# Experts' passes gathered in pairs from the first one, and what was spread over the first pass moved ahead of it

## The chip, the cores and the metric

The kernel runs on one core of a Trainium2 chip, in one launch. The metric is device time in microseconds (us) of one execution, from the first instruction to the last with what lies around them.

## The reference, cut to what matters

Two layers over 512 tokens of 1024 channels, all in float32. Each layer has a token mixer (layer 0 a Conformer convolution module of 31 taps, layer 1 a short gated convolution of 3 taps) and then a mixture of 32 experts in 4 groups: the best group, and in it the best two experts of each token. Both sublayers are wrapped in the same way:

```python
h = x * (1 + scale(c)) + shift(c)
x = layer_norm(ALPHA * x + (1 + gate(c)) * sublayer(h))
# the mixture's sublayer, with the tokens sorted by expert:
hid = silu(xblk @ w_gate[e]) * (xblk @ w_up[e])     # 1024 -> 512
y[tok] += weight * (hid @ w_down[e])                # 512 -> 1024
```

Every expert is used, so all its three matrices of 2 MB are read: 403 MB in the two layers, of 485 MB read in all.

## The kernel before

**Passes.** A layer's experts are taken in 14 passes of 128 slots (`PASSES`): a pass holds one to four experts in blocks of 32 slots, `(2, 2)` being two experts of 64 slots each. The experts are put on these places by their number of tokens (`perm`, L1062), but for experts 0 and 1, which always make pass 0, so that its weights can be loaded before the routing is known. Passes 1 and 13 have four experts, pass 2 one, pass 7 three, the others two.

**What a pass does** (L1214 on). A one-hot matrix of tokens against slots (`onehot`, L996) gathers the tokens: TensorE multiplies channels by tokens with it (`gather`, L1039), 16 products for two of the eight channel chunks, and ACT (L1043) and DVE (L1045) write the result with the mixture's scale and shift. Then 16 steps `t` of gate and up products (L1271), silu, four transposes (L1330), down products (L1346) in two halves `u`. The slots' routing weights come from four float32 products of the one-hot with `Wd` (`slot_weights`, L1132), and the one-hot's transpose from four transposes with a copy on ACT (`cmat`, L1122, L1125). With this transpose the next pass adds the result to the tokens (`combine`, L1150 and DVE L1142), two of its eight pieces at t = 4, 8, 12 and after.

**Gathers.** Pass 0 is gathered alone, from the float32 tokens in X (L1033). Passes 1 and 2, 3 and 4, ... 11 and 12 are gathered in pairs of 256 slots and pass 13 alone, both from a split of the tokens into a rounded high part `nh` (ACT L961) and the rest `nl` (DVE L957), in the faster float32r. Pass 0 is thus also where the four low parts are made, where all four gathers of the first pair stand (`ahead`, L1319), and where the mixture's scale and shift are turned into the other order of channels that the split has (`by_rows`, L275): two matrices built on POOL and DVE and eight products on TensorE (L292).

**Weights.** A ring of six buffers of 2 MB; SP issues the next unit's transfer when a buffer has been released (`done`, `pump`). A unit of pass 0 (`u_first`) holds gate and up of both experts for two chunks of channels, so that t runs gate, up, gate, up; in the other passes (`u_pass`) a unit holds four chunks of one matrix of two experts. A step's release stands after t = 3, 7, 11, 15 and after each half of the down products. The numbers of the experts from pass 1 on reach SP's registers by `ids` (L1089).

**The order of the work** is written out by hand: each engine runs its instructions in program order, the ones of `by_rows` and the DMA issues of ACT among them. Before pass 13, `beyond` (L1212) holds a branch for experts with more tokens than slots; it isn't taken, but every engine passes it.

**The mixer's end** (`Out.run`, L569): the output product in three float32r products for each k (L484 to L486), for its weights a high part on ACT and a low part on DVE (`fold`, `low`: L552, L558), then for each of four token groups q the layer norm (`ln`), transposes (`turn`, L895), copies (L903) and router products (`logits`, L910), and `choose` on DVE.

Of the kernel before, what the change touches and what calls it, by code (L numbers as in the profile page):

```python
# [62 lines left out]
def trunk_kernel(ctx: ExitStack, tc: tile.TileContext, x, c, ada_w, ada_b, a_w_in, a_b_in, a_w_dw, a_b_dw,  # L63
# [115 lines left out]
    def u_first(i, u):  # L179
        def f():  # L180
            t = R([128, 2, 2, 2, 512])
            for s, e in enumerate(experts(i, 0)):
                for z, w in enumerate((e_w_gate, e_w_up)):
                    nc.sync.dma_start(t[:, s, :, z], w[i, e, u * 256:(u + 1) * 256, :]
                                      .rearrange("o (k p) n -> p (o k) n", p=128))
            return t
        return f


# [18 lines left out]
    for i in range(DEPTH):  # L208
# [66 lines left out]
    def by_rows(aff, off):  # L275
        u, spread8 = W([128, 512]), W([128, KD, 2, 8])
        t8, div8, m8, mod8 = u[:, :240], u[:, 240:480], u[:, 480:481], u[:, 488:496]

        G.iota(t8, pattern=[[-8, 240]], base=8 * 112, channel_multiplier=1, **IOTA)
        V.tensor_scalar(div8, t8, 0.0, None, op0=OP.is_ge)  # L280
        V.scalar_tensor_tensor(div8, t8, 8.0, div8, op0=OP.is_lt, op1=OP.mult)
        V.tensor_mul(t8, t8, div8)
        V.tensor_reduce(m8, t8, axis=AX.X, op=OP.add)
        V.tensor_scalar(mod8, slot[:, :8], m8, None, op0=OP.is_equal)
        for z, a in enumerate((aff, off)):
            V.tensor_tensor(spread8[:, :, z], bc(a[:, :, None], [128, KD, 8]), bc(mod8[:, None, :], [128, KD, 8]),
                            op=OP.mult)

        def finish():
            p = P("b")  # L290
            for k in range(KD):
                PE.matmul(p[:, :16], div8[:, 112 - 16 * k:240 - 16 * k], spread8[:, k].rearrange("p z j -> p (z j)"),  # L292
                          start=k == 0, stop=k == KD - 1)
            r = T([128, 2, 8], F32, "aff8")
            S.activation(r.rearrange("p z j -> p (z j)"), p[:, :16], AF.Copy)
            return r
        return finish
# [242 lines left out]
    class Out:  # L540
# [28 lines left out]
        def run(self, uT, pre, uh, ul, extra, turn, copies, logits, choose, fill):  # L569
# [45 lines left out]
            for q in range(NQ):  # L615
# [226 lines left out]
    fold_rest()  # L842
    res = Out(grow, False)
# [27 lines left out]
    for i in range(DEPTH):  # L871
# [76 lines left out]
        res.run(uT, pre, nh, nl, None if i else add_bias, turn, copies, logits, choose, flex)  # L948


        def tokens(q):
            qs = slice(q * 128, (q + 1) * 128)
            return nh[:, :, qs], nl[:, :, qs], X[:, q, :].rearrange("p (n k) -> p k n", k=KD)

        def tokens_low(q):
            hi, lo, x = tokens(q)
            V.tensor_sub(lo, x, hi.bitcast(F32))  # L957

        for q in range(NQ):
            hi, lo, x = tokens(q)  # L960
            S.activation(hi, x, AF.Copy)  # L961
# [39 lines left out]
        def single(g, at, dt):  # L1001
            t = W([128, NQ, 128], dt)
            onehot(t, g, at)
            return t, None

        def pair(Q, at):
            if Q == NP // 2:
                return single(NP - 1, at, F32R)
            t = [W([128, 2, 256], F32R) for _ in range(2)]
            for h in range(2):  # L1010
                for j in range(2):
                    onehot(t[h][:, :, j * 128:j * 128 + 128], 2 * Q - 1 + j, at[:, 2 * h:2 * h + 2])
            return t

        def oh(Q, q, j=None):
            if ohs[Q][1] is None:
                return ohs[Q][0][:, q, :]
# [3 lines left out]
        def xe(Q, k, j=None):  # L1021
            r = xes[Q][k // 4][:, k % 4, :]
            return r if j is None or Q % (NP // 2) == 0 else r[:, j * 128:j * 128 + 128]

        def gather(Q, k0):
            p = P("c", (128, 2, 256))
            n = 128 if Q % (NP // 2) == 0 else 256
            for k in (k0, k0 + 1):  # L1030
                for q in range(NQ):
                    if Q == 0:
                        PE.matmul(p[:, k - k0, :n], X[:, q, k * 128:(k + 1) * 128], oh(Q, q), start=q == 0, stop=q == NQ - 1)  # L1033
                        continue
                    o = oh(Q, q)
                    if n == 128:
                        o = bc(o[:, None, :], [128, 2, 128])
                    for part, src in enumerate((nh, nl)):
                        PE.matmul(p[:, k - k0], src[:, k, q * 128:(q + 1) * 128], o, start=q == 0 and part == 0,  # L1039
                                  stop=q == NQ - 1 and part == 1)  # L1040
            affe, offe = maps[min(Q, 1)]
            k = k0
            S.activation(xe(Q, k), p[:, 0, :n], AF.Identity, bias=offe[:, k:k + 1], scale=affe[:, k:k + 1])  # L1043
            k = k0 + 1
            V.tensor_scalar(xe(Q, k), p[:, 1, :n], affe[:, k:k + 1], offe[:, k:k + 1], op0=OP.mult, op1=OP.add)  # L1045

        maps = [(aff, off)]

        ohs = [single(0, VW[:, 0], F32)]
        xes = [[W([128, 4, 128]) for _ in range(2)]]  # L1050

# [10 lines left out]
        V.tensor_scalar(perm, rank, kc[:, 1:2], None, op0=OP.is_equal)  # L1062

# [16 lines left out]

        t = by_expert(0)
        gather(0, 0)
        Vd = by_place(t, "Vd")

# [5 lines left out]

        nbf = W([1, 2, NE, 8])
# [26 lines left out]

        def cmat(ohq, C=None):
            p = P("c")  # L1120
            for q in range(NQ):
                PE.transpose(p[:, q * 128:(q + 1) * 128], ohq(q), ident)  # L1122
            if C is None:
                C = W([128, 512], F32R)
            S.activation(C, p, AF.Copy)  # L1125
            return C

        def slot_weights(ohq, e, kind):
# [4 lines left out]
            w = T([128, 5], F32, "ws", 4)  # L1133
            if n == 1:
                V.tensor_copy(w[:, 4:5], p[:, :1])
            else:
                V.scalar_tensor_tensor(w[:, :n], p[:, :n], 1.0, side[kind], op0=OP.mult, op1=OP.mult,
                                       accum_out=w[:, 4:5])
            return w[:, 4:5]
# [14 lines left out]
        def block(e, rest, eid, tiles):  # L1154
# [4 lines left out]
            w = slot_weights(lambda q: t[:, q, :].bitcast(F32), e, (4,))  # L1159
            cmat(lambda q: t[:, q, :].bitcast(F32), C)  # L1160
# [411 lines left out]
```

## Time and profile before

| | |
|---|---|
| three runs: median; lowest to highest | 3024.08 us; 1514.51 to 7848.31 us |
| the profiled execution: time, span | 1515.81 us, 1513.7 us |
| mean granted TensorE clock | 0.971 of 2.4 GHz |
| busy: PE, DVE, ACT, POOL | 94%, 48%, 23%, 17% of the span |
| passes 5 and 6 of layer 0: first gate product | 454.7 and 486.1 us |
| layer 0: experts' first gate product to last down product | 272.2 to 761.0 us |
| layer 1: the same | 1003.1 to 1492.7 us |

The span in 40 slices of 37.8 us (tenths; 9 is 90% or more), with what the DMA engines moved:

```profile
PE   5999889999999999998899989999899999999975
DVE  2699987532324333232157877563233333333315
DMA  8954435879999999999994655257999999999984
GB/s 296 396 204 171 167 111 175 323 296 421 419 378 405 404 421 420 421 421 418 357 279 153 203 200 178 105 223 282 423 421 415 402 384 421 421 421 420 421 360 156
```

The experts of layer 0 fill slices 8 to 20, those of layer 1 slices 27 to 39. TensorE is busy nearly everywhere; the DMA engines come to a ceiling of 421 GB/s in the experts' stretches alone. Where both are full, the rows of the releases and of the waits have to tell which sets the pace.

### The profile page before, as it was taken

To read this page: it belongs to the slowest core of one execution; us is meant where nothing else is said; L and a number is where in the kernel's file an instruction comes from. 1 tells how busy PE (TensorE), PEld (TensorE's weight loads), DVE (VectorE), ACT (ScalarE), POOL (GpSimd) and SP (SyncE) were. 2 spreads that over 40 slices of the span, in tenths; PEclk is the share of its full clock that TensorE was granted. 3 is DMA by queue.
4 is the path that set the end of the run, shared out by engine and by line. 5 is a ranking of instruction groups with operands and counts; after the bars stand their busy time and mean duration, and the time that the engine had idled before them with its cause. 6 is when DMAs were issued, how large, how long until landed. Compare 5 with 4: busy or idle time off the path is not lost. (4 is left out here: it accounts for less than half of the span.)

```text
span 1513.7 us, 21337 instructions
## 1 busy us (share of the span) xinstructions
PE 1416.6 (94%) x8424; PEld 769.3 (51%) x8424; DVE 725.2 (48%) x1298; ACT 341.3 (23%) x583; POOL 264.2 (17%) x275
## 2 busy tenths in 40 slices
PE   5999889999999999998899989999899999999975
PEld 3444467544544445443277777865354444444422
DVE  2699987532324333232157877563233333333315
ACT  1465565220111011110061222232001110011101
POOL 1399942050000000000025142002200000000002
PEclk8999999999999999999999999999999999999978
DMA  8954435879999999999994655257999999999984
GB/s 296 396 204 171 167 111 175 323 296 421 419 378 405 404 421 420 421 421 418 357 279 153 203 200 178 105 223 282 423 421 415 402 384 421 421 421 420 421 360 156
DMA packets 118851, 488.72 MB, mean 323 GB/s; under 512 B 12227, under 2 KB 45515, under 8 KB 71627
## 3 DMA queue, kind: packets, MB, share of 16 engines
q1 hardware_dynamic: 114443, 486.82, 81.4%
q8 instruction: 71, 1.16, 0.3%
q0 software_dynamic: 128, 0.04, 0.2%
q10 hardware_dynamic: 4160, 0.30, 0.2%
q14 instruction: 49, 0.40, 0.1%
HBM read 485.02 MB, written 2.10 MB: 322 GB/s over the span
## 5 line engine op out<-in xcount | busy, mean ns | idle before, releaser
L1271 PE MATMUL pa<-ring,w 128*32 128x512 f32 (+2 forms) x2624 | 430.6, 605 | 25.8 <-DMA ring<-in_e_w_up_dram 12.4
L1142 DVE TENSOR_TENSOR X<-X,pb 128x512 f32<-128x512 f32 x208 | 133.9, 683 | 263.8 <-PE pb L1150 263.2
L1271 PEld LDWEIGHTS pa<-ring,w 128*32 128x32 f32 (+2 forms) x2624 | 118.0, 120 | 273.5 <-issue 242.8
L1346 PE MATMUL pa<-ring,w 128*32 128x512 f32 (+2 forms) x1312 | 208.8, 601 | 8.7 <-DMA ring<-in_e_w_down_dram 7.1
L1346 PEld LDWEIGHTS pa<-ring,w 128*32 128x32 f32 (+2 forms) x1312 | 60.8, 120 | 133.4 <-issue 113.3
L1150 PE MATMUL pb<-w,w 128*128 128x512 f32 x416 | 128.2, 429 | 0.0
L765 PE MATMUL pa<-RB,ring 128*128 128x512 f32 x256 | 117.3, 616 | 4.8 <-DMA ring<-in_a_w_in_dram 2.7
L1366 DVE SCALAR_TENSOR_TENSOR w<-pa,ws,w 128x512 f32<-128x512 f32 x56 | 41.8, 750 | 163.3 <-PE pa L1346 160.7
L1150 PEld LDWEIGHTS pb<-w,w 128*128 128x128 f32 x416 | 71.0, 189 | 95.4 <-issue 81.8
L710 POOL TENSOR_TENSOR w<-w,w 128x512 f32<-128x512 f32 x80 | 104.8, 1309 | 57.1 <-ACT w L708 51.5
L1125 ACT ACTIVATE w<-pc 128x512 fp32r<-128x512 f32 x28 | 16.7, 597 | 429.6 <-PE pc L1122 429.6
L1039 PE MATMUL pc<-w,RB 128*128 128x256 f32 x448 | 111.4, 288 | 0.0
L1039 PE MATMUL pc<-w,RC 128*128 128x256 f32 x448 | 108.6, 278 | 0.0
L481 POOL TENSOR_TENSOR RC<-w,RB 128x512 fp32r<-128x512 f32 x8 | 10.9, 1382 | 440.0 <-ACT RB L480 440.0
L1039 PEld LDWEIGHTS pc<-w,RB 128*128 128x128 f32 x448 | 84.5, 189 | 2.6 <-issue 1.6
L1039 PEld LDWEIGHTS pc<-w,RC 128*128 128x128 f32 x448 | 84.1, 188 | 1.1
L765 PEld LDWEIGHTS pa<-RB,ring 128*128 128x128 f32 x256 | 49.4, 197 | 67.9 <-issue 62.4
L480 ACT ACTIVATE w<-w 128x512 fp32r<-128x512 f32 x58 | 36.6, 631 | 208.9 <-DVE w L1366 208.9
L724 DVE SCALAR_TENSOR_TENSOR pb<-RC,w,pb 128x512 f32<-128x512 f32 x126 | 83.6, 745 | 0.0
L1407 POOL TENSOR_TENSOR X<-X,w 128x512 f32<-128x512 f32 x3 | 4.9, 1619 | 428.9 <-ACT X L1406 428.9
L486 PE MATMUL pa<-RB,w 128*128 128x512 f32 x168 | 68.7, 409 | 8.8 <-DVE w L481 8.8
L1045 DVE TENSOR_SCALAR w<-pc,aff 128x256 f32<-128x256 f32 (+1 forms) x56 | 29.4, 525 | 91.3 <-ACT w L1043 91.3
(350 smaller groups left out, 1830.2 us busy)
## 6 DMA issues: line engine op xcount, KB each, us to landing
ring<-in_e_w_down_dram SPq DMA_DIRECT2D x120, 1024.0 KB, 15.6
ring<-in_e_w_gate_dram SPq DMA_DIRECT2D x120, 1024.0 KB, 12.1
ring<-in_e_w_up_dram SPq DMA_DIRECT2D x120, 1024.0 KB, 16.7
ring<-in_ada_w_dram SPq DMA_DIRECT2D x14, 2048.0 KB, 11.5
ring<-in_ada_w_dram SPq DMA_DIRECT2D x10, 1536.0 KB, 6.3
ring<-in_b_w_in_dram SPq DMA_DIRECT2D x24, 512.0 KB, 6.3
ring<-in_a_w_in_dram SPq DMA_DIRECT2D x8, 1024.0 KB, 8.0
ring<-in_e_w_gate_dram SPq DMA_DIRECT2D x16, 512.0 KB, 6.3
```

Of the source, the lines that this page charges most:

```text
L480: S.activation(hi, x, AF.Copy)
L486: PE.matmul(p, al, bh, start=False, stop=stop)
L710: G.tensor_add(vp, vp, z)
L724: V.scalar_tensor_tensor(t if j == TAPS - 1 else acc[n % 2], a, wj, acc[n % 2], op0=OP.mult, op1=OP.add)
L765: PE.matmul(p, w[:, k, h, s], hT[:, k, :], start=k == 0, stop=k == KD - 1)
L1039: PE.matmul(p[:, k - k0], src[:, k, q * 128:(q + 1) * 128], o, start=q == 0 and part == 0, stop=q == NQ - 1 and part == 1)
L1045: V.tensor_scalar(xe(Q, k), p[:, 1, :n], affe[:, k:k + 1], offe[:, k:k + 1], op0=OP.mult, op1=OP.add)
L1142: V.tensor_add(half(q, d), half(q, d), p)
L1150: PE.matmul(p, C[:, q * 128:(q + 1) * 128], ys[d][z], start=z == 0, stop=z == 1)
L1271: PE.matmul(pgu[z][a:b, :], xe(Q, k, j)[:, a:b], w[s][:, t % 4, :] if g else tiles[-1][:, s, k % 2, z, :], start=k == 0, stop=k == KD - 1)
L1346: PE.matmul(pd[d][a:b, :], hT[:, (2 * u + f) * 128 + a:(2 * u + f) * 128 + b], w[s][d][:, f, :], start=u + f == 0, stop=u + f == 2)
L1366: V.scalar_tensor_tensor(ys[d], pd[d], ws, GF[d], op0=OP.mult, op1=OP.mult)
```

## The change

Pass 0 is gathered with pass 1 as a pair, 2 with 3, and so on to 12 with 13, all from the split tokens. For that, pass 0's weights get the layout of the others (`u_first` goes), the low and high parts are made at the mixer's end and in the routing (`hook`), and pass 1's half of the first one-hot, which needs `Vd`, is built before the first gather. `by_rows` runs once for each layer at the mixer's end: two transposes, a copy on ACT and 16 small transfers issued by ACT. `slot_weights` and `cmat` become `slots_of`: one product for each token group in float32r gives the weights in two parts and each slot's token number, and DVE builds the transposed one-hot by comparing token numbers.

```diff
-    def u_first(i, u): ...
-            if g == 0:
-                todo += [u_first(i, u) for u in range(4)] + [u_pass(i, g, 4 + u) for u in range(2)]
-            elif g < NP - 1:
+            if g < NP - 1:
                 todo += [u_pass(i, g, j) for j in range(3 * n)]
...
     def by_rows(aff, off):
-        u, spread8 = W([128, 512]), W([128, KD, 2, 8])
...
+        p = P("b")
+        t = W([8, 2, 128])
         for z, a in enumerate((aff, off)):
+            PE.transpose(p[:8, z * 128:(z + 1) * 128], a, ident)
+        S.activation(t.rearrange("k z c -> k (z c)"), p[:8, :256], AF.Copy)
+        r = T([128, 2, 8], F32, "aff8")
+        for z in range(2):
             for k in range(KD):
+                S.dma_start(r[16 * k:16 * k + 16, z, :], t[k:k + 1, z, :].rearrange("o (a j) -> o a j", j=8))
+        return r[:, 0], r[:, 1]
...
                 ln(q, (lambda: copies(q - 2)) if q >= 2 else None)
+                if q < 3:
+                    hook("high", q)
             turn(2)
             copies(2)
             logits(0)
             logits(1)
+            hook("low", 0)
...
             turn(3)
             copies(3)
+            hook("high", 3)
+            hook("low", 1)
             logits(2)
             logits(3)
...
     fold_rest()
+    maps = by_rows(aff, off)          # layer 0
     res = Out(grow, False)
...
                 fold_router(1, rw, aff, off)()
+                maps = by_rows(aff, off)          # layer 1
                 res = Out(grow, True)
...
-        ohs = [single(0, VW[:, 0], F32)]
+        ohs = [pair(0, VW[:, 0], (0,))]
...
         V.tensor_scalar(perm, rank, kc[:, 1:2], None, op0=OP.is_equal)
+        hook("low", 2)
...
         t = by_expert(0)
-        gather(0, 0)
+        flex.finish()
+        if i == 0:
+            side_ada.finish()
         Vd = by_place(t, "Vd")
+        pair(0, Vd, (1,), ohs[0])
+        hook("low", 3)
...
         V.tensor_copy(ids[i], pid[:1, :NE])
+        gather(0, 0)
...
-        def cmat(ohq, C=None): ...
-        def slot_weights(ohq, e, kind): ...
+        def slots_of(ohq, e, kind, C=None):
             n = len(kind)
             p = P("c")
             for q in range(NQ):
-                PE.matmul(p[:, :n], ohq(q), Wd[:, q, e:e + n], start=q == 0, stop=q == NQ - 1)
+                PE.matmul(p[:, :4 * n], ohq(q), Wd[:, q, 4 * e:4 * e + 4 * n], start=q == 0, stop=q == NQ - 1)
...
+            V.tensor_copy(w[:, 9:10], p[:, 2:3])
+            if C is None:
+                C = W([128, 512], F32R)
+            for q in range(NQ):
+                V.tensor_scalar(C[:, q * 128:(q + 1) * 128], slot, 128.0 * q, w[:, 9:10], op0=OP.add, op1=OP.is_equal)
+            return w[:, 8:9], C
...
         for g, kind in enumerate(PASSES):
-            Q, j = (g + 1) // 2, (g + 1) % 2
+            Q, j = g // 2, g % 2
...
-                z, k = (t % 2, t // 2) if g == 0 else (t // 4 % 2, t // 8 * 4 + t % 4)
+                z, k = t // 4 % 2, t // 8 * 4 + t % 4
...
-                    if t in (1, 5, 9):
-                        gather(0, t // 4 * 2 + 2)
-                    if t in (2, 4, 6, 8):
-                        tokens_low(t // 2 - 1)
-                    if t == 3:
-                        rows8 = by_rows(aff, off)
...
+                    if t in (1, 4, 6):
+                        gather(0, {1: 2, 4: 4, 6: 6}[t])
...
             def ahead(n):
-                if Q < NP // 2:
...
-                    for k0 in (2 * n,) if Q == 0 else (4 * j + 2 * n,):
-                        gather(Q + 1, k0)
+                if Q + 1 < NP // 2:
+                    gather(Q + 1, 4 * j + 2 * n)
...
                         t = by_expert(1)
-                        ahead(2)
-                        Wd = by_place(t, "Wd")
-                        C = cmat(ohq)
+                        Wd = places(t)
                     else:
-                        ws = slot_weights(ohq, FIRST[g], kind)
-                        ahead(3)
+                        ws, C = slots_of(ohq, FIRST[g], kind)
```

`places` makes `Wd` with four columns for an expert: the weight's high and low part, and the token's number twice.

## Rows read from the trace of the kernel before

**Rows 1.** Windows: us, busy PE, PEld, DVE, ACT, POOL, clock, DMA share, GB/s
```profile
415.00:520.00 105.00, 105.00 (x740) 47.69 (x743) 36.81 (x68) 12.26 (x21) 0.00 (x0) 1.00 0.97 394
520.00:715.00 195.00, 188.55 (x1236) 87.54 (x1229) 65.02 (x121) 20.42 (x36) 0.00 (x0) 0.99 1.01 421
1140.00:1250.00 110.00, 110.00 (x781) 51.21 (x780) 39.20 (x75) 12.82 (x22) 0.00 (x0) 1.00 0.98 399
```

**Rows 2.** Timeline of SP: start, length, the issue of weights (two transfers a unit)
```profile
278.07 0.89 SPq L174 DMA_DIRECT2D ring<-in_e_w_gate_dram  x2
322.69 2.01 SPq L174 DMA_DIRECT2D ring<-in_e_w_up_dram  x4
1052.40 1.33 SPq L174 DMA_DIRECT2D ring<-in_e_w_up_dram  x2
```

**Rows 3.** Timeline of SP, around the branch of layer 1
```profile
1435.67 0.86 SPq L174 DMA_DIRECT2D ring<-in_e_w_gate_dram  x2
1453.16 2.38 SPq L174 DMA_DIRECT2D ring<-in_e_w_up_dram  x4
```

**Rows 4.** Timeline of PE in pass 5: slots' weights, transposes, two gather products
```profile
469.62 0.95 PE L1132 MATMUL pc<-Wd,w 128*128 128x2 f32 x8
470.43 0.63 PE L1122 MATMUL pc<-ident,w 128*128 128x128 f32 x4
...
474.75 0.28 PE L1039 MATMUL pc<-w,RB 128*128 128x256 f32 x1
474.87 0.28 PE L1039 MATMUL pc<-w,RC 128*128 128x256 f32 x1
```

**Rows 5.** Timeline of DVE in layer 0: perm; a low part; four one-hots
```profile
268.19 0.23 DVE L1062 TENSOR_SCALAR w<-rank,r_kc 32x32 f32<-32x32 bf16 x1
...
277.02 2.02 DVE L957 TENSOR_TENSOR RC<-X,RB 128x1024 fp32r<-128x1024 f32 x1
...
290.56 1.41 DVE L996 TENSOR_TENSOR w<-slot,Vd 128x256 fp32r<-128x256 f32 x4
```

**Rows 6.** Timeline of PE in pass 0, layer 0: two steps; by_rows
```profile
272.24 1.94 PE L1271 MATMUL pa<-ring,w 128*64 128x512 f32 x8
...
292.48 1.96 PE L292 MATMUL pb<-w,w 128*128 128x16 f32 x16
```

**Rows 7.** Timeline of ACT at layer 0's mixer end: copies; high parts
```profile
249.43 1.06 ACT L903 ACTIVATE w<-pb 128x512 f32<-128x512 f32 x2
...
257.21 8.03 ACT L961 ACTIVATE RB<-X 128x1024 fp32r<-128x1024 f32 x4
```

**Rows 8.** Timeline of PE there: turn(2)
```profile
250.75 1.03 PE L895 MATMUL pb<-ident,X 128*128 128x128 f32 x8
```

**Rows 9.** Timeline of PE: the end of an idle time in layer 0's mixer
```profile
228.25 0.79 PE L484 MATMUL pb<-w,RB 128*128 128x512 f32 x1 [3.00 <-ACT RB L574]
```

**Rows 10.** Window around it
```profile
223.00:234.00 11.00, 7.62 (x18) 5.43 (x19) 9.44 (x11) 6.72 (x12) 8.18 (x6) 0.53 0.70 251
```

**Rows 11.** Timelines: small transfers' issues on ACT and SP
```profile
148.78 0.42 ACTq L259 DMA_DIRECT2D w<-in_r_w_group_dram  x1
149.24 0.59 ACTq L260 DMA_DIRECT2D w<-in_r_w_expert_dram  x1
...
3.59 0.29 SPq L233 DMA_DIRECT2D w<-in_a_ln_g_dram  x1
```

**Rows 12.** Timelines of PE and ACT, layer 0: router product; silu
```profile
185.79 3.37 PE L267 MATMUL pb<-w,affB 128*128 128x36 f32 x16 [1.30 <-DVE affB L464]
...
193.49 0.81 ACT L860 ACTIVATE w<-w,colP 128x512 f32<-128x512 f32 x1 [4.36 <-DVE w L859]
```

**Rows 13.** The same of layer 1: fold(0) on ACT; router product on PE
```profile
920.31 1.15 ACT L552 ACTIVATE w<-ring 128x512 fp32r<-128x512 f32 x2
...
931.36 1.87 PE L267 MATMUL pb<-w,affB 128*128 128x36 f32 x16
```

**Rows 14.** DMA issues: count, size, median us to landing
```profile
w<-in_r_w_group_dram ACTq DMA_DIRECT2D x2, 16.0 KB, 2.5
```

More of the change, by code (lines that the diff above doesn't have):

```diff
@@ L176, in u_pass @@
         return f
[L179 to L187, printed above, removed]
     def u_last(i, d):
@@ L566, in early, with run @@
             self.u[k] = t
-        def run(self, uT, pre, uh, ul, extra, turn, copies, logits, choose, fill):
+        def run(self, uT, pre, uh, ul, extra, turn, copies, logits, choose, fill, hook):
             def u(k):
@@ L945, in by_group, with hook @@
             return t.rearrange("p q (g e) -> p q g e", g=NG)
-        res.run(uT, pre, nh, nl, None if i else add_bias, turn, copies, logits, choose, flex)
-        def tokens(q):
+        def hook(what, q):
             qs = slice(q * 128, (q + 1) * 128)
[L953 to L961, printed above, removed]
+            hi, lo, x = nh[:, :, qs], nl[:, :, qs], X[:, q, :].rearrange("p (n k) -> p k n", k=KD)
+            if what == "high":
+                S.activation(hi, x, AF.Copy)
+            else:
+                V.tensor_sub(lo, x, hi.bitcast(F32))
+        res.run(uT, pre, nh, nl, None if i else add_bias, turn, copies, logits, choose, flex, hook)
         cnt = P("b")
@@ L999, in onehot, with pair @@
                 o += n * c
[L1001 to L1009, printed above, removed]
+        def pair(Q, at, passes=(0, 1), t=None):
+            t = t or [W([128, 2, 256], F32R) for _ in range(2)]
             for h in range(2):
-                for j in range(2):
-                    onehot(t[h][:, :, j * 128:j * 128 + 128], 2 * Q - 1 + j, at[:, 2 * h:2 * h + 2])
+                for j in passes:
+                    onehot(t[h][:, :, j * 128:j * 128 + 128], 2 * Q + j, at[:, 2 * h:2 * h + 2])
             return t
         def oh(Q, q, j=None):
-            if ohs[Q][1] is None:
-                return ohs[Q][0][:, q, :]
             r = ohs[Q][q // 2][:, q % 2, :]
@@ L1022, in xe @@
             r = xes[Q][k // 4][:, k % 4, :]
[L1023 removed]
+            return r if j is None else r[:, j * 128:j * 128 + 128]
         def gather(Q, k0):
+            if k0 == 0:
+                xes.append([M([128, 4, 256]) for _ in range(2)])
             p = P("c", (128, 2, 256))
[L1029 removed]
             for k in (k0, k0 + 1):
                 for q in range(NQ):
[L1032 to L1037, printed above, removed]
                     for part, src in enumerate((nh, nl)):
[L1039 removed]
+                        PE.matmul(p[:, k - k0], src[:, k, q * 128:(q + 1) * 128], oh(Q, q), start=q == 0 and part == 0,
                                   stop=q == NQ - 1 and part == 1)
[L1041 removed]
+            affe, offe = maps
             k = k0
[L1043 removed]
+            S.activation(xe(Q, k), p[:, 0], AF.Identity, bias=offe[:, k:k + 1], scale=affe[:, k:k + 1])
             k = k0 + 1
[L1045 to L1050 removed]
+            V.tensor_scalar(xe(Q, k), p[:, 1], affe[:, k:k + 1], offe[:, k:k + 1], op0=OP.mult, op1=OP.add)
+        xes = []
+        ohs = [pair(0, VW[:, 0], (0,))]
         rk = W([NE, 3, NE])
@@ L1079, in by_place, with places @@
             return d
+        def places(t):
+            p = P("a", (128, NQ, 128))
+            for q in range(NQ):
+                PE.matmul(p[:, q, :NE], t[:, q * 128:(q + 1) * 128], perm, start=True, stop=True)
+            n = W([128, NQ, NE])
+            G.iota(n, pattern=[[128, NQ], [0, NE]], base=0, channel_multiplier=1, **IOTA)
+            d = W([128, NQ, 4 * NE], F32R)
+            z = d.rearrange("p q (e z) -> p q e z", z=4)
+            V.tensor_copy(z[:, :, :, 0], p[:, :, :NE])
+            V.tensor_sub(z[:, :, :, 1], p[:, :, :NE], z[:, :, :, 0].bitcast(F32))
+            V.tensor_copy(z[:, :, :, 2], n)
+            V.tensor_copy(z[:, :, :, 3], n)
+            return d
         t = by_expert(0)
-        gather(0, 0)
+        flex.finish()
+        if i == 0:
+            side_ada.finish()
         Vd = by_place(t, "Vd")
+        pair(0, Vd, (1,), ohs[0])
+        hook("low", 3)
         pid = P("a")
@@ L1245, in trunk_kernel @@
                     o += wide
[L1246 removed]
+            ohq = lambda q: oh(Q, q, j)
             if g == NP - 1:
@@ L1264, in trunk_kernel @@
             for t in range(2 * KD):
-                z, k = (t % 2, t // 2) if g == 0 else (t // 4 % 2, t // 8 * 4 + t % 4)
-                if t % 4 == 0 and g == 0:
-                    tiles.append(unit())
-                elif t % 4 == 0:
+                z, k = t // 4 % 2, t // 8 * 4 + t % 4
+                if t % 4 == 0:
                     w = [piece(t // 4 * ns + s) for s in range(ns)]
@@ L1319, in ahead @@
             def ahead(n):
-                if Q < NP // 2:
-                    first = g == max(0, 2 * Q - 1)
-                    if first and n == 0:
-                        xes.append([M([128, 4, 256]) if Q + 1 < NP // 2 else W([128, 4, 128]) for _ in range(2)])
-                    for k0 in (2 * n,) if Q == 0 else (4 * j + 2 * n,):
-                        gather(Q + 1, k0)
+                if Q + 1 < NP // 2:
+                    gather(Q + 1, 4 * j + 2 * n)
             ahead(0)
@@ L1371, in trunk_kernel @@
             pend = (C, ys)
-            if j == 1 and Q + 2 <= NP // 2:
+            if j == 1 and Q + 2 < NP // 2:
                 ohs.append(pair(Q + 2, Vd))
```

58 lines of the change are left out of this document (12 added, 46 removed).

## Prediction

> **What bounds the kernel now.** I read the windows by stage first. In the experts' stretches the DMA engines have a ceiling of 421 GB/s: they hold it for the 195 us of layer 0's passes 6 to 13, with TensorE nearly full beside them, while in the earlier passes 3 to 6 TensorE is full without a gap and the DMA engines fall to 394 GB/s (layer 1: 399) [rows 1]. So two limits lie close together. A pass of two experts is 12.6 MB, 29.9 us at the ceiling; TensorE's own time for one is some 31.4 us, the distance from pass 5 to pass 6 in the table. Passes 3 to 6 are TensorE's, the rest is the transfers': pass 7 with its three experts uses up the ring's lead, and from there no faster TensorE ends a layer sooner. What the transfers lose is small: 105 x (1 - 394/421) = 6.7 us in layer 0, 110 x (1 - 399/421) = 5.7 us in layer 1 [rows 1].
>
> The queue of SP shows how a layer starts. The first buffer is released at 278.07, a step of pass 0; but the transfers come to the ceiling only with the releases at 322.69 (layer 1: 1052.40), when pass 1's first four steps are done and two buffers come free at once [rows 2]. Before that a buffer comes free more slowly than a transfer of 5 us lasts, so those early releases may move without moving the end; the time that counts is pass 1's. At a layer's end SP stands at the branch: it issued its last unit before it at 1435.67 and the next at 1453.16, when all that was under way had landed [rows 3]. From there the rest is fixed: 12.6 MB and the last products. A layer's time is thus: when pass 1 releases, plus the stream at 421 GB/s, plus what TensorE holds the stream back in passes 3 to 6, plus a fixed tail. Outside the experts' stretches the mixers' chains count in full.
>
> **The passes.** The slots' weights and the transposes take 1.4 us of TensorE in a pass [rows 4]. Four float32r products take their place; a gather's follow each other by 0.12 us with the same 128 columns to load [rows 4], so 0.5 us, and 0.9 us is saved. The copy on ACT goes to DVE as four comparisons and two small instructions, about 1.2 us by the one-hots' price [rows 5]; DVE is 35% busy there [rows 1], and the next pass's combine, the first to read the result, comes after the down products. Nothing for that; without the cover 1.2 us a pass. Over passes 1 to 6 TensorE gains 5.4 us, which the stream can use as far as it was held back. In passes 7 to 13 the same 0.9 us, and the two gathers that pass 12 loses, end in a longer wait for weights: nothing. Only behind the last landing of layer 1 does the 0.9 us count once more.
>
> **The start of the experts.** Before, the first products stand at 272.24 [rows 6], and their gather needed no `perm`. After it, DVE has behind `perm` (done at 268.4) a low part (2.0), small additions and a copy (0.9, by the 0.2 to 0.3 us of such instructions), two one-hots (0.7) and another low part (2.0) [rows 5], to 274.0. The last products of the gather wait for that one: 1.2 us more, 0.7 us for the eviction, so 275.9, 3.7 us late. In layer 0 one more wait: the high part of q = 2 (8.03/4 = 2.0 us) now stands on ACT ahead of the copies of 249.43, and turn(2) at 250.75 needs the banks that they empty [rows 7, 8]: 1.9 us on the routing. In layer 1 ACT has that room; its low parts cost about 0.5 us there. Since TensorE idles longer before the first gather, I add 1.7 us for a stretch at the lower clock, as around an idle time of 3 us before, where the mean fell to 0.53, most of it at 1.2 GHz instead of 2.4 [rows 9, 10]. And t = 2 now waits for its own eviction, 0.7 us. Sum: 8.0 us in layer 0, 6.8 us in layer 1. Pass 0 then gives back the products of `by_rows` (2.0) [rows 6], two of four gathers of the next pair (32 x 0.12 = 3.8), and 0.9 of slots' work, with 0.6 us of `flex` transposes that fall into the wait in layer 0: 7.3 and 6.7 us. So pass 1's release comes 0.7 us later in layer 0 and 0.1 us later in layer 1. Bounds: 3 us either way, as the lower clock and DVE's order fall. The stream's gain is then the smaller of what it lost and what TensorE gave: 5.4 - 0.7 = 4.7 us in layer 0, and 5.3 us in layer 1.
>
> **The map's transfers.** Two transposes, a copy, then 16 issues on ACT, which runs in order. Nothing in the trace is a 512-byte transfer across partitions; the nearest are ACT's own issues, 0.42 and 0.59 us long and 0.46 apart, and SP's of 4 KB at 0.29 [rows 11]. I take 0.40 us each with the gap, nearest to ACT's shorter one, so 6.4 us; the ends 0.33 and 0.63 give 5.3 and 10.1 us. In layer 0 the router product ends at 189.2; transposes and copy to 190.0, issues to 196.4, fold(0) behind them 1.1, and silu starts at 197.5 instead of 193.49 [rows 12, 13]. DVE and ACT hand each other every k from there, and DVE hardly rests until the output product's last k: 4.0 us late, all on the path. In layer 1 it is worse. ACT was ahead there: it did fold(0) at 920.31, 11 us before the router product ended at 933.2 [rows 13]. Now its copy waits for that product's PE queue, so fold(0) starts at 933.2 + 0.8 + 6.4 = 940.4, and DVE's low part, which until now came some 0.5 us after the router product, follows at 941.0: 7.2 us late, and TensorE, idle for that long, comes back at the lower clock as in the same rows: 1.3 us more. 8.5 us.
>
> The transfers must land too: the Trainium skill, "DMA: Bandwidth & Descriptors", section "Rules for kernel authors", says to coalesce many small transfers, since under 64 KB one pays mostly overhead, which its section on the anatomy of one DMA puts at about 2.0 us each. The trace has 2.5 us to landing for ACT's 16 KB [rows 14], but the next issue came 0.46 us after it [rows 11]: the overhead overlaps. By the row the 16 cost 6.4 us; one after the other they would cost 16 x 2.5 = 40 us. Landed they are needed only at the first gather, some 60 us later.
>
> **The sum**, against the profiled execution of 1515.8 us (span 1513.7 and 2.1 around it): layer 0 +4.0 - 4.7; layer 1 +8.5 - 5.3 - 0.9: 1517.4, say **1517 us**. The median of the three runs, 3024 us, is twice that execution and not the kernel's own time; the lowest, 1514.51, agrees with it. I forecast no change that can be measured: a difference under 2% is about what a measurement of this kernel can't tell from none.
>
> **Rivals.**
> 1. *The early releases count, each of them.* If the stream ran at the ceiling from the first release on, the whole delay would pass: 8.0 + 6.8 - 0.8 = 14 us, 1531 us. For it: the first transfers do come later. Against it: the ceiling is reached only from 322.69 on [rows 2]. 0.12.
> 2. *The issues on ACT are hidden*, as small transfers cost ACT's queue little, or the chains behind have slack: without 12.5 us, 1505 us. Against it: no slack in DVE's row of work. 0.13.
> 3. *TensorE is the bound throughout.* Then all its savings count: 0.9 x 28 + the float32 gathers, 4 x 2.0 x 2, + 2.0 x 2 of by_rows, 45 us less; with 12.5 us of issues 1483 us. Against it: 421 GB/s for 195 us. 0.03.
> 4. *Slower: ACT's transfers go one by one*, each waiting out a landing of 2.5 us [rows 14]: by_rows then holds ACT 40 us in each layer, 33.6 us more than counted, 1517 + 67 = 1584 us. It decides from about 1.3 us for an issue on (16 x 2 x 0.9 more makes 29 us). Against it: the 0.46 us between two issues [rows 11]. 0.05. The Trainium skill's rule on small transfers points this way; with its 2.0 us in place of 2.5 this rival would give 1568 us, an estimate from that page.
>
> My forecast has 0.64, with its own spread: 5 us down (issues at 0.33, DVE's chain with slack), 13 us up (issues at 0.63, 3 us at each start). Rivals 1 and 2 fall at its ends, so the range is 1502 to 1533, with rivals 3 and 4 and some 0.1 outside. Faster by over 2% (under 1485) 0.04, slower (over 1546) 0.06, the rest no change.
>
> **What would show it.** Right: 16 issues on ACT some 0.4 us apart behind the router product, with silu 4 us and layer 1's first low part 7 us late; the first release in layer 0 6 to 8 us late and pass 1's within 1 us; middle passes of 30.5 us in the stretch that fell to 394 GB/s, now near 421; longer waits for weights from pass 8 on. Wrong: middle passes that stay at 31.4 us because DVE's new work holds the next pass; transfers of the map that land one by one; or the stream under 421 GB/s after pass 7, which would make TensorE the bound.

## The result, and the profile after

The changed kernel takes 1526.34 us in the median of four runs (1525.19 to 1528.89). Of the four runs of the kernel before beside it two are far longer than one execution (3024.08 and 7848.31 us); the other two took 1513.87 and 1514.51 us. By these two the change costs 12.2 us, a ratio of 1.0080; the ratio on record is 1.0087, 95% interval 1.0064 to 1.0109. So it is slower by 0.8 to 0.9%, clear of noise. I had forecast 1517 us, a sum of 1.6 us more than before, and no change that can be measured. The profiled execution took 1526.11 us, 10.3 more than the 1515.81 of before; spans 1524.3 and 1513.7.

The map's transfers first (the map is the mixture's scale and offset, which `by_rows` turns into the other order of channels). ACT's timeline in layer 0 (start, length, engine, line, operation, tiles; in brackets the idle time before and what ended it):

```profile
189.85 0.37 ACT L267 ACTIVATE w<-pb 8x256 f32<-8x256 f32 x1 [1.85 <-PE pb L266]
190.25 10.42 ACTq L271 DMA_DIRECT2D aff<-w  x16
200.72 1.15 ACT L527 ACTIVATE w<-ring 128x512 fp32r<-128x512 f32 x2 [10.50 <-DMA aff<-w]
201.78 0.80 ACT L841 ACTIVATE w<-w,colP 128x512 f32<-128x512 f32 x1
```

The 16 issues hold ACT for 10.42 us, 0.65 each, not the 6.4 us of my sum. `fold(0)` (L527) stands behind them, and the first silu (L841) comes at 201.78 instead of 193.49 [rows 12]. The output product ends 8.6 us later against the router product's start; its last products, before and after:

```profile
250.52 0.39 PE L486 MATMUL pa<-w,RC 128*128 128x512 f32 x1
```

```profile
259.12 0.40 PE L461 MATMUL pa<-w,RC 128*128 128x512 f32 x1
```

In layer 1 it is the same, on ACT, on DVE (the low part; the first line is the kernel before) and on PE:

```profile
939.25 10.40 ACTq L271 DMA_DIRECT2D aff<-w  x16
949.70 1.15 ACT L527 ACTIVATE w<-ring 128x512 fp32r<-128x512 f32 x2 [10.48 <-DMA aff<-w]
```

```profile
933.75 1.29 DVE L558 TENSOR_TENSOR w<-ring,w 128x512 fp32r<-128x512 f32 x2
```

```profile
950.36 1.29 DVE L533 TENSOR_TENSOR w<-ring,w 128x512 fp32r<-128x512 f32 x2 [11.23 <-ACT w L527]
```

```profile
936.66 1.87 PE L254 MATMUL pb<-w,affB 128*128 128x36 f32 x16
951.42 0.80 PE L459 MATMUL pb<-w,w 128*128 128x512 f32 x1 [12.67 <-ACT w L455]
```

`fold(0)` ran at 920.31, ahead of the router product at 931.36 [rows 13]; now it follows it. The low part started 2.4 us after the router product's start, now 13.7 us after it, and TensorE stands idle for 12.67 us.

The passes did what was forecast. PE and DVE in pass 5, then the windows that answer to [rows 1] (us, busy PE, PEld, DVE, ACT, POOL, clock, DMA share, GB/s):

```profile
475.82 0.51 PE L1105 MATMUL pc<-w,w 128*128 128x8 f32 x4
```

```profile
477.03 0.88 DVE L1118 TENSOR_SCALAR w<-slot,ws 128x128 fp32r<-128x128 f32 x4
```

```profile
415.00:520.00 105.00, 105.00 (x721) 48.96 (x723) 42.29 (x98) 10.10 (x17) 0.00 (x0) 1.00 1.01 415
520.00:705.00 185.00, 182.77 (x1188) 80.14 (x1180) 70.60 (x148) 17.45 (x29) 0.00 (x0) 1.00 1.01 420
1140.00:1250.00 110.00, 110.00 (x718) 51.34 (x721) 44.74 (x101) 10.32 (x18) 0.00 (x0) 1.00 1.01 420
```

The stream of weights, 394 and 399 GB/s in these stretches before, is now near its ceiling. Pass 5 to pass 6 is 30.5 us instead of 31.4.

The start of the experts: PE's wait for the banks of turn(2), its first gate product, and the releases on SP in both layers.

```profile
260.84 1.14 PE L876 MATMUL pb<-ident,X 128*128 128x128 f32 x8 [1.32 <-ACT w L884]
...
286.66 1.12 PE L1248 MATMUL pa<-ring,w 128*64 128x512 f32 x2 [0.66 <-ACT w L1004]
```

```profile
295.06 8.77 SPq L174 DMA_DIRECT2D ring<-in_e_w_gate_dram  x4
...
332.06 2.03 SPq L174 DMA_DIRECT2D ring<-in_e_w_up_dram  x4
...
1068.66 2.17 SPq L174 DMA_DIRECT2D ring<-in_e_w_up_dram  x4
...
1464.26 2.39 SPq L174 DMA_DIRECT2D ring<-in_e_w_up_dram  x4
```

Pass 1's release comes at 332.06 (before 322.69) and 1068.66 (1052.40) [rows 2], and SP leaves layer 1's branch at 1464.26 instead of 1453.16 [rows 3]. Where each kernel stood at the same marks (us from the span's start, from the timelines; router product and passes by their start). The columns from the third on are experiments of the next section: before_map, before_slots, pairs_two, map_two, slots_late. Each column is one execution, and 21 executions of the kernel before ran from 1509.8 to 1519.2 us, so a difference of 1 or 2 us between columns is not shown by it:

| | before | changed | map alone | slots alone | pairs, 2 transfers | all, 2 transfers | slots, map late |
|---|---|---|---|---|---|---|---|
| layer 0: router product | 185.8 | 185.7 | 185.2 | 184.9 | 185.4 | 184.4 | 185.4 |
| output product ends | 250.9 | 259.5 | 257.9 | 249.9 | 250.4 | 248.8 | 250.4 |
| pass 0 starts | 272.2 | 286.7 | 279.0 | 271.0 | 277.6 | 276.0 | 272.9 |
| pass 1 starts | 315.9 | 325.3 | 319.7 | 314.1 | 317.1 | 314.2 | 314.5 |
| experts end | 761.0 | 765.6 | 763.6 | 754.8 | 762.2 | 754.5 | 752.9 |
| layer 1: router product | 931.4 | 936.7 | 934.1 | 925.4 | 931.5 | 927.0 | 923.5 |
| output product ends | 982.5 | 999.9 | 997.0 | 976.5 | 986.5 | 981.8 | 974.6 |
| pass 0 starts | 1003.1 | 1025.0 | 1016.0 | 997.6 | 1011.7 | 1006.8 | 996.2 |
| pass 1 starts | 1045.6 | 1061.9 | 1056.4 | 1042.2 | 1051.0 | 1043.7 | 1036.1 |
| experts end | 1492.7 | 1503.3 | 1502.8 | 1484.7 | 1498.7 | 1485.5 | 1479.1 |

Read down the second column against the first: +8.6 at the mixer's end of layer 0, +9.4 at pass 1, +4.6 at the experts' end; in layer 1 +5.3, +17.4, +16.3, +10.6. The mixers lose 8.6 and 12.1 us; everything else of the change together gives 10.1 back.

### The profile page after: what moved, and what is told of

It reads as the page before. It is cut to its first block, busy times and chain, and to the rows that moved or that the text cites. A ratio compares the mean times of both kernels' runs of the same rounds, so it can differ in the third digit from the quotient of the medians.

```text
span 1524.3 us, 20672 instructions
## 1 busy us (share of the span) xinstructions
PE 1390.1 (91%) x8044; PEld 736.9 (48%) x8044; DVE 743.0 (49%) x1426; ACT 326.7 (21%) x547; POOL 264.1 (17%) x275
## 5 line engine op out<-in xcount | busy, mean ns | idle before, releaser
L1248 PE MATMUL pa<-ring,w 128*32 128x512 f32 (+2 forms) x2624 | 442.2, 605 | 32.0 <-DMA ring<-in_e_w_up_dram 18.7
L1248 PEld LDWEIGHTS pa<-ring,w 128*32 128x32 f32 (+2 forms) x2624 | 121.0, 120 | 286.0 <-issue 230.2
L1307 PE MATMUL pa<-ring,w 128*32 128x512 f32 (+2 forms) x1312 | 208.7, 600 | 10.1 <-DMA ring<-in_e_w_down_dram 7.0
L1130 PE MATMUL pb<-w,w 128*128 128x512 f32 x416 | 131.5, 438 | 0.7 <-DVE X L1122 0.5
L1307 PEld LDWEIGHTS pa<-ring,w 128*32 128x32 f32 (+2 forms) x1312 | 60.9, 120 | 134.6 <-issue 112.4
L745 PE MATMUL pa<-RB,ring 128*128 128x512 f32 x256 | 114.2, 602 | 5.2 <-DMA ring<-in_a_w_in_dram 3.1
L1000 PE MATMUL pc<-w,RB 128*128 128x256 f32 x448 | 114.5, 294 | 1.7 <-DVE w L972 1.7
L1000 PE MATMUL pc<-w,RC 128*128 128x256 f32 x448 | 111.7, 284 | 0.7 <-DVE RC L935 0.7
L455 ACT ACTIVATE w<-w 128x512 fp32r<-128x512 f32 x58 | 36.6, 631 | 251.0 <-DVE w L1324 250.9
L1004 ACT ACTIVATE w<-pc,aff 128x256 f32<-128x256 f32 x56 | 31.6, 565 | 264.1 <-PE pc L1000 264.1
L1276 ACT ACTIVATE w<-pa 128x512 f32<-128x512 f32 x28 | 16.7, 597 | 309.1 <-PE pa L1248 309.1
## 6 DMA issues: line engine op xcount, KB each, us to landing
ring<-in_e_w_up_dram SPq DMA_DIRECT2D x128, 1024.0 KB, 15.8
```

Of the source, the lines that this page charges most:

```text
L745: PE.matmul(p, w[:, k, h, s], hT[:, k, :], start=k == 0, stop=k == KD - 1)
L1000: PE.matmul(p[:, k - k0], src[:, k, q * 128:(q + 1) * 128], oh(Q, q), start=q == 0 and part == 0, stop=q == NQ - 1 and part == 1)
L1004: S.activation(xe(Q, k), p[:, 0], AF.Identity, bias=offe[:, k:k + 1], scale=affe[:, k:k + 1])
L1130: PE.matmul(p, C[:, q * 128:(q + 1) * 128], ys[d][z], start=z == 0, stop=z == 1)
L1248: PE.matmul(pgu[z][a:b, :], xe(Q, k, j)[:, a:b], w[s][:, t % 4, :], start=k == 0, stop=k == KD - 1)
L1307: PE.matmul(pd[d][a:b, :], hT[:, (2 * u + f) * 128 + a:(2 * u + f) * 128 + b], w[s][d][:, f, :], start=u + f == 0, stop=u + f == 2)
```

## The experiments

Ratios are to the kernel before, run beside each experiment on the same chip, where it had medians of 1514.0 to 1515.5 us.

**map_two.** The changed kernel, with the permutation of each of scale and offset as one transfer.

```diff
         for z in range(2):
-            for k in range(KD):
-                S.dma_start(r[16 * k:16 * k + 16, z, :], t[k:k + 1, z, :].rearrange("o (a j) -> o a j", j=8))
+            S.dma_start(r[:, z, :], t[:, z, :].rearrange("k (a j) -> k a j", j=8))
```

> The changed kernel with the map's permutation as 2 transfers in a layer (one for the scale, one for the offset) instead of 16; the bytes and the pieces of 32 bytes stay the same. Theory A: an issue holds ACT for 0.65 us whatever is in it, and this stands in full on the path at both mixers' ends. Then ACT is held 1.3 us instead of 10.4; layer 0's first silu is back at 193.5 instead of 201.8 (8.3 us), layer 1's first low part comes at about 941 instead of 950.4 (9.2 us): 17.5 us less than the 1526.3 of the changed kernel, 1509 us. Theory B: the time goes by pieces (128 in each transfer now, 16 before), not by issues: ACT is held as long as before, 1526 us.

Measured: 1509.51 us, ratio 0.9966 (0.9952 to 0.9980). Theory A. ACT in layer 0:

```profile
188.92 1.87 ACTq L270 DMA_DIRECT2D aff<-w  x2
190.84 1.15 ACT L526 ACTIVATE w<-ring 128x512 fp32r<-128x512 f32 x2 [1.95 <-DMA aff<-w]
191.90 0.80 ACT L840 ACTIVATE w<-w,colP 128x512 f32<-128x512 f32 x1
```

The first issue, with 128 pieces, is 1.21 us long, the second 0.62, as long as one with 16 pieces; the pair holds ACT for 1.87 us, not the 1.3 of the theory. Silu stands 7.5 us behind the router product: 7.7 before, 16.1 in the changed kernel. The same change with 2 issues in place of 16 is faster than the kernel before.

**map_sp.** The changed kernel with the 16 transfers on SP's queue.

```diff
-                S.dma_start(r[16 * k:16 * k + 16, z, :], ...)
+                nc.sync.dma_start(r[16 * k:16 * k + 16, z, :], ...)
```

> The changed kernel with its 16 transfers in a layer issued by SP instead of ACT, at the same place. Theory A: the loss is that ACT is held with the folded weights behind it; on SP nothing stands behind them that the mixer's end needs, so both mixers are as with 2 transfers: layer 0's silu on time, layer 1's output product about 3.7 us late: 1509 us. Rival: SP waits there for TensorE's transposes and issues the units of weights behind them 10 us late; the ring is short of what the output product reads, and the end is where it was: 1520 to 1526 us.

Measured: 1507.75 us, ratio 0.9950 (0.9931 to 0.9969). Theory A.

```profile
189.73 10.98 SPq L271 DMA_DIRECT2D aff<-w  x16
200.82 0.52 SPq L124 DMA_DIRECT2D ring<-in_ada_w_dram  x1
```

SP pays the same price, 0.69 us a transfer with one stall in it, and nothing that the mixer's end needs stands behind. So it isn't the transfers that cost the mixers 20.7 us, it is the queue that they were given to.

**before_map.** The kernel before with the map's 16 transfers alone (`by_rows` as in the change).

```diff
     fold_rest()
+    maps8 = by_rows(aff, off)      # the 16 transfers; the same behind layer 1's router product
...
-        maps = [(aff, off)]
+        maps = [(aff, off), maps8]
...
-                    if t == 3:
-                        rows8 = by_rows(aff, off)
-                    elif t == 13: ...
```

> The kernel before with one part of the change alone: the map permuted by 16 transfers on ACT at the mixer's end, so that the two matrices and eight products of pass 0 go; pairs, token parts and slots as before. Theory A: silu 8.6 us late in layer 0, the output product 12.1 us late in layer 1, and pass 0 gives 2.0 us back in each layer: 1514.2 + 8.6 + 12.1 - 4.0 = 1531 us. Theory D: the changed kernel's late mixers come from another part of the change, and the ring of weights, which runs ahead in the meantime, takes such a delay up: within 5 us of 1514.

Measured: 1526.18 us, ratio 1.0076 (1.0057 to 1.0095): this one part is as slow as the whole change. The mixers lose 7.6 and 11.8 us; from their ends to the experts' ends 4.4 us come back in each layer, not the 2.0 that I had counted: 3.2 and 3.7 by pass 1's start, of which 3.0 and 2.1 in pass 0 itself (in layer 0 a wait of 0.9 us for DVE went there too), the rest behind it. To that extent theory D holds as well: a part of a delay is taken up.

**before_slots.** The kernel before with `slots_of` and `places` in place of `slot_weights` and `cmat` (pass 0 in float32, as its one-hot is).

```diff
-                    ws = slot_weights(ohq, FIRST[g], kind)
-                    C = cmat(ohq)
+                    ws, C = slots_of(ohq, FIRST[g], kind)
```

> The kernel before with one part of the change alone: slots' weights and token numbers from one product, the transposed one-hot by comparisons on DVE. Theory A: TensorE saves 0.9 us in a pass, 5.4 us over passes 1 to 6 of each layer, all of which the stream of weights can use, and 0.9 us behind the last landing: 1514.2 - 11.7 = 1502.5 us, with passes 3 to 6 at 30.5 us instead of 31.4. Rival: the comparisons on DVE hold the next pass, or the stream cannot use the time: passes of 31.4 us or the same end of the experts, 1513 us.

Measured: 1506.03 us, ratio 0.9942 (0.9924 to 0.9959). The passes are 30.5 us and layer 0 gains 5.3 us from router product to experts' end, as forecast; layer 1 gains only 2.0. In its profiled execution pass 0 of layer 1 ran for a part at the lower of TensorE's two levels, as the windows over it show (here, and in the kernel before):

```profile
997.00:1042.00 45.00, 45.00 (x263) 26.81 (x263) 21.25 (x55) 7.28 (x15) 0.25 (x1) 0.93 0.72 264
```

```profile
1003.00:1045.00 42.00, 42.00 (x262) 25.18 (x261) 19.40 (x47) 8.35 (x16) 0.00 (x0) 1.00 0.75 279
```

A clock of 0.93 over 45 us is 3 us at most; pass 0 is 2.2 us longer (44.7 for 42.5). What brought it down in this execution no run tells, and the rest of the shortfall against the forecast of 6.3 stays open. In the one execution of slots_late, below, layer 1 gains 5.7 us.

**pairs_two.** The changed kernel with 2 transfers, and `slot_weights` and `cmat` as before: the diff of before_slots backwards, on top of map_two.

> The changed kernel with the map by 2 transfers at the mixer's start and the slots' weights and transposes as before: pairs and token parts alone. Against the 1509.5 us with the slots in one product. Theory A: the passes are 31.4 us again and the stream of weights falls back to some 395 to 400 GB/s in passes 3 to 6, which costs 4.8 us in layer 0, 5.5 in layer 1 and 0.9 at the end: 1509.5 + 11 = 1520 us, later than the kernel before: pairs and token parts lose time by themselves. Rival: pairs from the first pass gain by themselves, and slots and pairs fill the same gap in the stream: 1510 to 1514 us.

Measured: 1519.92 us, ratio 1.0029 (1.0012 to 1.0047). Theory A: passes of 31.4 us, and

```profile
415.00:520.00 105.00, 105.00 (x740) 48.70 (x742) 37.52 (x74) 12.26 (x22) 0.00 (x0) 1.00 0.96 392
```

again 392 GB/s. Pairs and token parts gain nothing by themselves; the stream's gain is the slots'. That they lose 5.9 us by themselves, as the theory has it, is not shown: 3.9 of them stand in layer 1's mixer (55.0 us from router product to output product's end, 51.1 before), where the 2 transfers still stand ahead of `fold(0)`. From the mixers' ends to the experts' ends the trace shows 1.7 and 2.0 us lost, in one execution. Pairs with the old slots and no transfers in the mixer were not run.

**map_late.** The 16 transfers of the changed kernel in the routing, ahead of `choose`.

```diff
             logits(3)
+            hook("map", 0)       # maps = by_rows(aff, off), no longer at the mixer's start
             choose()
```

> The changed kernel with the same 16 transfers in a layer, moved from the mixer's start of the output product to the routing, ahead of the choice of experts on DVE, where ACT has 16 us with three small instructions in it. Theory A (held issues on the path are the loss): both mixers get their 8.6 and 12.1 us back, and the two copies that stand behind the issues on ACT in the routing come some 3 us late, which the first gather pays in each layer: 1526.3 - 20.7 + 6 = 1512 us. Theory C: the small transfers cost what they cost wherever they stand (the routing's chain has no room either): the whole 10 us comes back at the first gather, 1525 us.

Measured: 1517.69 us, ratio 1.0023 (1.0007 to 1.0040): between the two. The mixers came back (their ends are 0.6 us before and 2.0 behind the kernel before), but the routing had less room than I read from it. ACT and PE in layer 0:

```profile
262.17 13.09 ACTq L271 DMA_DIRECT2D aff<-w  x16
275.30 0.38 ACT L368 ACTIVATE w<-pc 128x256 f32<-128x256 f32 x1 [13.16 <-issue]
```

```profile
275.74 1.12 PE L375 MATMUL pc<-ident,w 128*128 128x128 f32 x4 [7.60 <-ACT r_kc L1020]
```

13.09 us for the 16, since from one issue to the next it took 1.4 to 2.0 us at three places, and a wait of 7.60 us on TensorE, not 3. In layer 1 the 16 took 10.32 us at the same place. What held the three is not shown: the DMA engines were 62% busy there and 54% in layer 1, but SP's 16 in map_sp had such a gap too, 1.4 us in each layer, with the DMA engines 3% busy.

**two_late**, **two_late_h2.** map_late with 2 transfers; then also the high part of the third token group behind that group's copies.

```diff
-                if q < 3:
+                if q < 2:
                     hook("high", q)
             turn(2)
             copies(2)
+            hook("high", 2)
```

> The changed kernel with the map by 2 transfers and these moved to the routing, ahead of the choice of experts. With the 2 transfers at the mixer's start layer 1 still stood 3.7 us later at its output product's end than at its router product, against the kernel before (layer 0: 0.7 us earlier). Theory A (what is left in layer 1 is ACT's first folded weights, which had been made ahead of the router product and now wait behind the map): the 3.7 us come back, the 1.9 us of issues fit into the 6.6 us between the last router product's copies and the next work of ACT: 1509.5 - 3.7 = 1506 us. Rival: the routing has no room for them either, and an issue waits there for the weights' transfers: 1509 us.

> The version with 2 late transfers, with one more edit: the high part of the third token group is made behind the copies of that group's transposes on ACT, not ahead of those of the second. The prediction had 1.9 us for this wait in layer 0; the changed kernel shows 1.3 us of idle TensorE there. Theory A: layer 0's experts start 1.3 us earlier and the end moves by as much, layer 1 stays: 1.3 us less than the version without the edit. Rival: the high part is then late for the low part on DVE, and the first gather waits for it: no change or up to 2 us more.

Measured: 1508.14 us, ratio 0.9957 (0.9942 to 0.9973), and 1505.48 us, ratio 0.9941 (0.9923 to 0.9959). In the traces both edits do their part: layer 1 takes 51.1 us from router product to output product's end, as before the change (map_two 54.8), and from the output product's end to the first product of the experts' counts layer 0 takes 14.9 us with the second edit, 15.8 without. In the times the intervals of map_two and of these two overlap from each to the next, so that neither edit alone is shown; pass 1 of layer 0 was 47.3, 44.6 and in map_two 45.3 us long, a spread larger than what was sought.

**slots_two**, **slots_late.** before_slots, and the map by 2 transfers in place of `by_rows`' products: at t = 10 of pass 0, or ahead of `choose`.

```diff
-                    if t == 3:
-                        rows8 = by_rows(aff, off)
-                    elif t == 13: ...
+                    if t == 10:                        # slots_two
+                        maps.append(by_rows(aff, off))
...
         def choose():
+            mapped.append(by_rows(aff, off))           # slots_late
```

> The kernel before with two parts of the change, pairs and token parts left as they were: slots' weights and token numbers in one product, and the map by 2 transfers, issued at t = 10 of pass 0, where ACT has nothing else until silu. Against the 1506.0 us with the slots alone, pass 0 loses the eight products of the two matrices (2.0 us) and gains two transposes (0.3): 1.7 us in each layer. Theory A (pass 1's release sets when the stream starts): 1506.0 - 3.4 = 1502.6 us. Rival (pass 0 and 1 wait for weights anyway): 1506 us.

Measured: 1513.92 us, ratio 0.9998 (0.9987 to 1.0010), worse than both theories. ACT and PE in pass 0 of layer 0:

```profile
288.12 1.87 ACTq L283 DMA_DIRECT2D aff<-w  x2
...
299.48 1.02 ACT L1030 ACTIVATE w<-pc,aff 128x256 f32<-128x256 f32 x2 [7.57 <-DMA aff<-w]
```

```profile
301.28 6.16 PE L1341 MATMUL pa<-ring,w 128*64 128x512 f32 x16 [4.68 <-DVE w L1327]
```

The issues are short, but the landing took some 10 us among the weights' transfers; the first pair's gather waited for the map, and TensorE 4.68 us behind it (layer 1: 4.6).

> The kernel before with the slots in one product and the map by 2 transfers, issued in the routing ahead of the choice of experts instead of at t = 10 of pass 0; pairs and token parts as before. Theory A (at t = 10 the transfers stood among the weights' and took 10 us to land, so that the first pair's gather, ACT behind it and TensorE waited 4.7 us in each pass 0): in the routing the ring is full and little else is under way, the landing is over long before the gather, and pass 0 gives 1.7 us in each layer against the slots alone: 1506.0 - 3.4 = 1502.6 us. Rival (the time is lost wherever ACT issues them, or pass 0 waits for weights in their place): 1506 to 1514 us.

Measured: 1503.68 us, ratio 0.9931 (0.9909 to 0.9953), the lowest median of all, 11.8 us under the kernel before beside it. It lies nearer to theory A (1502.6) than to the rival, but its interval overlaps those of before_slots and of two_late_h2, so that a gain over the slots alone is not shown. Nor does the theory's reason hold. The window over the two issues (260.87 to 262.73):

```profile
258.00:272.00 14.00, 11.31 (x127) 8.65 (x127) 6.58 (x33) 9.58 (x10) 0.00 (x0) 0.88 0.97 366
```

The DMA engines were 97% busy there too. How long this landing took the trace doesn't tell; nobody needs the map before 297.73, 35 us behind the issues, and there the product is what ACT waits for, not the map:

```profile
297.73 0.56 ACT L1033 ACTIVATE w<-pc,aff 128x256 f32<-128x256 f32 x1 [2.37 <-PE pc L1029]
```

## Why the prediction was off

The step that failed: "I take 0.40 us each with the gap, nearest to ACT's shorter one, so 6.4 us". An issue took 0.65 us with its gap, 10.4 us for the 16, just above the upper end that I had kept (0.63, 10.1 us). At that end my sum is 1517.4 + 2 x 3.7 = 1524.8 us, 1.5 under the median measured. The mechanism was right: the queue that it stood in, the work behind it, and that all of it is on the path. The size was off, once in each layer: map_two and map_sp show it by taking the hold away, before_map by adding nothing else. With it went "I forecast no change that can be measured": the interval is 0.2% to either side, so that 0.8% is measured well, and "a difference under 2% is about what a measurement of this kernel can't tell from none" was wrong. Of the two rows of ACT in [rows 11], the shorter was no nearer to a 512-byte transfer than the longer.

By the terms of the sum:

- **The map's transfers**: forecast +4.0 and +8.5 us, measured +8.6 and +12.1. Of the 8.2 us beyond the forecast 8.0 are the issues' own (10.4 for 6.4, twice), and the 8.2 are nearly the whole of the 9.0 by which the spans miss it (10.6 against 1.6).
- **The passes**: slots on TensorE 0.51 us as forecast, on DVE 1.2 us hidden. From the mixer's end to the experts' end layer 0 gains 4.0 us (forecast 4.7), layer 1 6.8 (forecast 5.3 + 0.9). pairs_two shows that this is the slots' work.
- **Where the stream takes over**: the prediction read the window from 520 to 715 us as passes 6 to 13; it is passes 7 to 12 (517.4 to 710.3), and passes 9 to 11 became shorter by the same 0.9 us (31.3 to 30.5). The sign "longer waits for weights from pass 8 on" didn't come: from 520 to 704 us TensorE's waits for weights are (us in all, times, longest)

```profile
PE pa L1248 <- DMA ring<-in_e_w_up_dram: 0.5, 1, 0.5
```

From pass 1's start to pass 13's the changed kernel gains 12.4 us in layer 0, and 4.8 of them are left at the experts' end: pass 13 takes 58.3 us instead of 50.7. The end moved with SP's leaving the branch, 4.6 us later in both (before, and changed):

```profile
724.38 2.02 SPq L174 DMA_DIRECT2D ring<-in_e_w_up_dram  x4
```

```profile
729.02 2.05 SPq L174 DMA_DIRECT2D ring<-in_e_w_up_dram  x4
```

So the transfers do set the end, as predicted, but the gain of TensorE is lost in the last pass and not from pass 8 on.

- **The start of the experts**: the first product came 5.8 us later than the mixer's delay in layer 0 and 4.5 in layer 1, where the parts of my sum up to it made 7.3 and 6.1; pass 0 gave back 5.0 and 5.6. Pass 1's start is thus 0.8 us late and 1.1 early beside the mixers' delay, forecast 0.7 and 0.1 late. The clock in the first gather and step was lower for longer than my 1.7 us had it (0.52 of 2.4 GHz over 14 us in layer 0, nearly all of it at 1.2 GHz; the window is below; 0.88 from 262 to 276 us before), and the waits on DVE were shorter (0.77 and 0.35 us). Of the sum for layer 1, 6.8 us, its parts make only 6.6 (3.7, 0.5, 1.7 and 0.7).

```profile
276.00:290.00 14.00, 11.58 (x46) 7.59 (x44) 10.38 (x35) 2.89 (x6) 0.00 (x0) 0.52 0.60 253
```

- **The early releases don't count** held: layer 0's first release was 17.0 us late (8.6 from the mixer, 8.4 of its own; I had said 6 to 8, and had not added the mixer's delay to it), and at the experts' end 4.6 us were left.
- **Rivals.** TensorE throughout and a gain from hidden issues are out. "ACT's transfers go one by one" is out: 0.65 us apart, each landed 1.7 us after its issue in the median:

```profile
aff<-w ACTq DMA_DIRECT2D x32, 0.5 KB, 1.7
```

Two readings beside the sum were off as well. `fold(0)` at 920.31 stood 11 us before the router product's start, and 13 before its end. And the 2.0 us that the prediction takes from the Trainium skill stand in a section on transfers issued from GpSimd; ACT's landed after 1.7 us here.

What the prediction named, the issues on ACT as the price that decides, was nonetheless the right place. The Trainium skill, "DMA: Bandwidth & Descriptors", section "Rules for kernel authors", says to coalesce many small transfers. This case agrees: 2 for 16 gave 17 us (1526.3 to 1509.5), and what was saved was the time of the issues. The Trainium skill, on the same page in "Issuing engines are not separate DMA queues", calls the time that a sequencer takes to start a transfer usually small beside the transfer. Here it was not small: 0.60 us beside 1.7 to landing, and moving the 16 from ACT to SP gave the same gain as making them 2 (1507.8 and 1509.5 us).

The pieces can't simply be added: in the kernel before the slots alone gain 8.2 us and the map alone loses 11.9; pairs with 2 transfers lose 5.9, but they have a part of the map in them. With the pairs in place the slots gain 10.4 us (pairs_two to map_two). They fill the gap in the stream that TensorE leaves it, in either kernel. Pairs move the start of pass 0 back by 5.3 us in layer 0, with the mixer as long as before.

## What to carry to other kernels

Price a small transfer by what the issuing engine's queue loses, not by its bytes: here 0.60 to 0.65 us for each issue, times their number, charged to whatever stands behind them in program order. Ask first whether a pattern of many can be two, then whether another queue has nothing urgent behind it, then when its landing is needed and what else will be landing at that time. And where two rows of the same kind differ by half and nothing says which is the nearer, make the whole sum at both.

## What was not expected of the hardware

- Issues cost more than pieces: the same 256 pieces of 32 bytes held ACT for 10.4 us in 16 issues and for 1.87 us in 2. One issue with 16 pieces was 0.60 us long on ACT and 0.59 on SP; with 128 pieces the second of a pair took 0.62, the first 1.15 to 1.21, in every pair on record. Why the first is longer is not shown.
- The landing of a small transfer took longer where more was under way: the same 512 bytes took 1.7 us in the mixers (DMA engines 2% busy) and 4.6 in the median in map_late's routing (54 to 62%), 7.2 at most; 4 KB took some 10 us among the weights in pass 0 (288 to 300 in slots_two, where 385 GB/s moved).

```profile
aff<-w ACTq DMA_DIRECT2D x32, 0.5 KB, 4.6
```

- In pass 13 TensorE waits 7 to 13 us for weights and their issue in every version, and what is gained ahead of the branch on TensorE alone is in part lost there: the changed kernel starts it 3.1 us earlier than before in layer 0 and ends it 4.6 later.
